# Gate and up side by side through Strassen's seven products in an encoder layer's two feed-forward blocks

## The chip, the cores and the metric

One NeuronCore of a Trainium2 chip runs the whole kernel. The metric is device time in microseconds (us) of one launch. TensorE (PE) multiplies matrices and writes its sums to PSUM, eight banks of 128 partitions x 512 fp32 in this kernel's use; VectorE (DVE) and ScalarE (ACT) do elementwise work; GpSimd (POOL) has a little of it; SyncE (SP) issues nearly all transfers.

## The reference

One encoder layer over 256 tokens of width 2048, in fp32: a feed-forward half-step, a mixer (attention and a Fourier branch), and a second feed-forward half-step. The two feed-forward steps are what the change is about:

```python
h = x + 1/2 * RMSNorm_post(SwiGLU(RMSNorm_pre(x)))     # D_MODEL = 2048, D_FF = 5632

def _rms_norm(x, g):
    y = xf * lax.rsqrt(jnp.mean(xf * xf, axis=-1, keepdims=True) + EPS)
    return y * g

def _swiglu(x, w_gate, w_up, w_down):
    return (jax.nn.silu(x @ w_gate) * (x @ w_up)) @ w_down
```

## The kernel before, in words

**Split products.** Every fp32 factor is cut into a high part (rounded to the fp32r type, by a copy on ACT, line 101) and a low part (the rest, by a subtraction on DVE, line 102); both lines are the helper `split`. A product is three matmuls (`mm3`, lines 106 to 108): high x high, high x low, low x high. The token side (128x128) is the stationary operand, the weight side (128x512) the moving one.

**Tokens.** 256 tokens are two tiles, t = 0 and 1. `u[t]` holds the transposed, gained but not yet normed input of a block, high and low part, 16 k-tiles of 128x128 each. The norm factor `rs[t]` is a number for each token and is applied after the product.

**Weights.** A weight piece is two k-tiles of 128x512: 512 KB, loaded into one of 5 raw buffers (`wraw`), split into one of 6 ring slots (`wring`). A ring slot comes free when the last matmul that reads it is done, a raw buffer when its split is done.

**The feed-forward loop (`ffn`).** The inner width 5632 is 11 blocks f of 512. For each f, `col_block` makes the gate product (16 k-tiles x 2 token tiles x 3 matmuls = 96 matmuls) and then the up product (96 more), each into two PSUM tiles `pc`. ACT takes the Silu of the gate (L445), DVE multiplies it by up (L447): `h`. After that `row_block` of the block before, f - 1, runs (96 matmuls for the four column parts of the down product into PSUM tiles `pr`, added to `y` by DVE at L219). Ahead of its fourth part, `turn_h` puts in eight transposes of `h` on PE (L177) into `pt`, which `split` turns into `hTh` and `hTl`, the stationary operands of the next `row_block`. The last block goes through `last_rows`, with the norm after the block and the transposed input of the next stage in an order written out by hand.

**What sets the order.** The kernel is traced in program order; a planner that runs ahead of time with its own estimates of durations then fixes the order of each engine's instructions and of the transfer queue, and hands out buffers. It takes what is ready, the earlier traced first. `tc.issue_after(ins)` pins instructions behind `ins` on `ins`'s engine, for work that would be ready too soon.

**Buffers.** `b8` has 8 buffers of 8 KB a partition for whole-width tiles (`y`, `h`, gains, mixer tiles); `upool` holds the four tiles of `u`; `chunk` has 3 pairs of 4 KB (`hT` and others); `wk` has 8 of 2 KB. PSUM is two pools, `pmm` with 5 banks for sums and `ptr` with 3 for transposes and small products.

Of the kernel before, what the change touches and what calls it, by code (L numbers as in the profile page):

```python
# [10 lines left out]
F32 = mybir.dt.float32  # L11
# [7 lines left out]
P = 128  # L19
D = 2048  # L20
# [25 lines left out]
SPARE_NEXT = ("b8", None, None, None)  # L46
B8 = 8
CH = 3
# [6 lines left out]
def encoder_layer(  # L55
    ctx: ExitStack,
    tc: tile.TileContext,
    x, xgT,
    f1_gate, f1_up, f1_down, f1_post,
    mix_pre, w_in, w_f, b_gate, q_g, k_g, w_ao, w_fo, w_fn, w_out, mix_post,  # L60
    f2_pre, f2_gate, f2_up, f2_down, f2_post,
    rope_cos, rope_sin, dft_pos, dft_ch, dft_ones, dft_mid, ident_in,
# [7 lines left out]
    b8 = pool("b8", B8)  # L70
    upool = pool("upool", 1)
# [51 lines left out]
    def pieces(src, spare=None):  # L123


        whole = {}

        def part(k0):
            if spare in (None, "chunk"):
                return piece(src, k0, WP, (chunk, "ch_hi", "ch_lo") if spare else None)  # L130
            if not whole:
                for c in ("h", "l"):
                    shape = [P, CK, NB]
                    whole[c] = big("w" + c, F32R, shape) if spare == "b8" else \
                        upool.tile(shape, F32R, tag=f"u{c}1", name=f"w{c}u")
# [38 lines left out]
    def transpose4(src, hi_dst, lo_dst):  # L174
        pt = ptr.tile([P, 4, P], F32, tag="tr", name="pt")
        for j in range(4):
            T.transpose(pt[:, j, :], src[:, j * P:(j + 1) * P], ident[:])  # L177
        split(hi_dst, lo_dst, pt[:])
# [5 lines left out]
    def new_u(t):  # L184
        return tuple(upool.tile([P, KD, P], F32R, tag=f"u{c}{t}", name=f"u{c}{t}") for c in "hl")

# [241 lines left out]

    def ffn(u, rs, wg, wu, wd, y, tail, gate0, w_next=None, early=()):

        nblk = F // NB
        prev = None
        for f in range(nblk):
            if f == 4:
                norm, nxt = tail()
            if f == 0:
                pg = gate0()
            else:
                pg = col_block(u, wg, f)
            pu = col_block(u, wu, f, between=early if f == 0 else ())  # L440
            ch = new_chunk("hT")
            hs = []
            for t in range(NT):
                sg = work("sg")
                A.activation(sg[:], pg[t][:], AF.Silu, scale=rs[t][:, 0:1])  # L445
                h = work("h")
                V.scalar_tensor_tensor(out=h[:], in0=pu[t][:], scalar=rs[t][:, 0:1], in1=sg[:],  # L447
                                       op0=ALU.mult, op1=ALU.mult)
                hs.append(h)

            def turn_h(ch=ch, hs=hs):
                for t in range(NT):
                    ts = slice(t * P, (t + 1) * P)
                    transpose4(hs[t], ch[0][:, :, ts], ch[1][:, :, ts])

            if prev is None:
                turn_h()
            else:
# [33 lines left out]

    def residual(t):
        h[t] = big(f"h{t}")
        load(h[t][:], x[t * P:(t + 1) * P, :])
        junk = big("junk8")
        ssq = small("ssx", 1)
        A.activation(junk[:], h[t][:], AF.Square, accum_out=ssq[:])
        rs[t] = rsqrt(ssq[:], 1, 1.0 / D, f"r{t}")

    y = [big(f"y{t}") for t in range(NT)]

    def tail():
# [3 lines left out]
    pk, nxt = ffn(u, rs, f1_gate, f1_up, f1_down, y, tail, gate0, w_in[4],  # L507
                  early=[lambda t=t: residual(t) for t in range(NT)])
    u, rs = nxt.u, nxt.rs
# [56 lines left out]
    def fold_tokens(b):  # L566

        a, e, o = work("ua"), work("ue"), work("uo")
        A.activation(a[:], cbs(nxt.y[0], b), AF.Copy, scale=rs[0][:, 0:1])
        for dst, op in ((e, ALU.add), (o, ALU.subtract)):  # L570
            V.scalar_tensor_tensor(out=dst[:], in0=cbs(nxt.y[1], b), scalar=rs[1][:, 0:1], in1=a[:], op0=ALU.mult, op1=op)
        bs = slice(4 * b, 4 * b + 4)
        for n, src in enumerate((e, o)):
            pt = ptr.tile([P, 4, P], F32, tag="tr", name="pt")
# [47 lines left out]
    def fold_f(k):  # L622

        if k == 0:
            pfold[0] = pmm.tile([P, NB], F32, tag="mm", name="pe")
            pfold[1] = ptr.tile([P, NB], F32, tag="tr", name="pe")
        if k + F_AHEAD < KD:
# [33 lines left out]
    def fourier_positions(b):  # L661

        zh, zl = workr("zh", [P, EW]), workr("zl", [P, EW])
        split(zh[:], zl[:], zs[b])
        pa = ptr.tile([P, NB], F32, tag="tr", name="pa")
# [9 lines left out]
        po = ptr.tile([P, NB], F32, tag="tr", name="pa")  # L675
# [12 lines left out]
    def fourier_channels(b, i, a):  # L688
# [3 lines left out]
        if j == 0:  # L692
            foT.append(new_chunk("foT"))
            pmid[0] = ptr.tile([P, NB], F32, tag="tr", name="pn")
        pb = ptr.tile([P, NB], F32, tag="tr", name="pb")
        c = slice(i * WO, (i + 1) * WO)
# [34 lines left out]
    def attn_scores(j, ch, t, ps):  # L731
# [3 lines left out]
        for hh in range(2):  # L735
            sc = ptr.tile([P, 2, S], F32, tag="tr", name="sc")
            for i in range(2):
# [16 lines left out]
    def attn_parts(j, ps, ch):  # L754
# [3 lines left out]
        def turn_p(hh, i):  # L758
            pt = ptr.tile([P, NT, S], F32, tag="tr", name="pt")
            for kt in range(NT):  # L760
# [6 lines left out]
        def values(hh, i, ph, pl):  # L767
            if i == 0:
                po[hh] = ptr.tile([P, 2, S], F32, tag="tr", name="po")
            js = slice(j * HD, (j + 1) * HD)  # L770
# [143 lines left out]

    y = [big(f"yf{t}") for t in range(NT)]

    def store(t, lo, n):
        nc.sync.dma_start(out[t * P:(t + 1) * P, lo:lo + n], h2[t][:, lo:lo + n])

    ffn(nxt.u, nxt.rs, f2_gate, f2_up, f2_down, y,  # L920
        lambda: (PostNorm(y, h2, bcast(f2_post, "gpost3"), 0.5, store), None), lambda: pg, early=[nxt.finish])

# [80 lines left out]


def _rows(w):
    k, n = w.shape
# [40 lines left out]
```

## Time and profile before

| | |
|---|---|
| median of 3 runs | 2079.43 us (2076.99 to 2079.51) |
| the profiled execution | 2076.99 us, span 2075.2 us, granted TensorE clock 0.999 |
| PE busy | 2053.8 us (99%), 9466 matmuls and transposes |
| DVE, ACT busy | 1317.2 us (63%), 1008.1 us (49%) |
| POOL busy | 50.9 us (2%) |
| moved by DMA | 411.11 MB, mean 198 GB/s |
| stages | first feed-forward block to about 745 us, mixer to about 1340 us, second feed-forward block to the end |

Busy time is a sum over the span; the length of a matmul record is its latency, and consecutive ones overlap, so PE's rate is read from the distance between starts.

### The profile page before, as it was taken

What the parts mean: (1) busy time and instruction counts of PE and PEld (TensorE: products, weight loads), DVE (VectorE), ACT (ScalarE), POOL (GpSimd) and SP (SyncE); (2) the same over time, 40 slices, a digit from 0 to 9 for tenths busy, and PEclk for the clock granted to TensorE, in tenths of its full rate; (3) what the DMA queues carried; (4) which work ended last, traced back from release to release, by engine and by line L of the source; (5) the groups of instructions that cost most, each with busy time, mean ns of one, the idle gap of its engine ahead of it and who ended that gap; (6) DMA issues with size and microseconds to landing.
All of it is one profiled execution on the core that took longest, in us unless ns stands there. A gap on an engine that the chain in (4) does not pass through costs nothing.

```text
span 2075.2 us, 25220 instructions
## 1 busy us (share of the span) xinstructions
PE 2053.8 (99%) x9466; PEld 1702.6 (82%) x9466; DVE 1317.2 (63%) x1682; ACT 1008.1 (49%) x1336; POOL 50.9 (2%) x46
## 2 busy tenths in 40 slices
PE   9999999999999999999999999999999999999998
PEld 7888888888888878888888888788888888888886
DVE  6545555555555698887877895864555555555556
ACT  7444444444444556556666654555444444444443
POOL 0000000000000020100000000200000000000002
PEclk9999999999999999999999999999999999999999
DMA  8665555555655686964555557466565555655553
GB/s 320 216 222 189 190 191 193 191 189 187 194 193 190 214 260 203 263 199 140 191 191 182 186 183 274 164 192 205 192 196 189 193 190 186 195 191 190 193 193 103
DMA packets 117867, 411.11 MB, mean 198 GB/s; under 512 B 12872, under 2 KB 19024, under 8 KB 116336
## 3 DMA queue, kind: packets, MB, share of 16 engines
q1 hardware_dynamic: 113392, 405.36, 59.3%
q0 software_dynamic: 4352, 4.13, 1.4%
q8 instruction: 74, 1.21, 0.2%
q14 instruction: 49, 0.40, 0.1%
HBM read 405.25 MB, written 4.19 MB: 197 GB/s over the span
## 4 chain that ended last, share of the span: by engine, by line
PE 94%; DVE 4%; DMA 1%; ACT 1%; issue 0%; SPq 0%; DVEq 0%; ACTq 0%
PE pc L107 19%; PE pc L108 19%; PE pc L106 19%; PE pr L106 10%; PE pr L107 10%; PE pr L108 10%; PE pt L177 1%; DVE wlo L102 1%; DMA raw<-in_w_fo 1%; DVE h L390 0%; PE pe L106 0%; PE pe L108 0%; PE pe L107 0%; PE pt L762 0%; PE pf L108 0%
## 5 line engine op out<-in xcount | busy, mean ns | idle before, releaser
L102 DVE TENSOR_TENSOR wlo<-raw,whi 128x1024 fp32r<-128x1024 f32 (+1 forms) x711 | 866.5, 1222 | 669.7 <-ACT whi L101 668.3
L101 ACT ACTIVATE whi<-raw 128x1024 fp32r<-128x1024 f32 (+1 forms) x711 | 751.2, 1059 | 874.8 <-PE pc L108 527.2
L106 PE MATMUL pc<-whi,uh 128*128 128x512 f32 x1840 | 719.3, 391 | 1.3 <-ACT uh L485 1.3
L107 PE MATMUL pc<-wlo,uh 128*128 128x512 f32 x1840 | 717.0, 390 | 2.2 <-DVE wlo L102 2.2
L108 PE MATMUL pc<-whi,ul 128*128 128x512 f32 x1840 | 717.2, 390 | 1.9 <-DVE ul L102 1.9
L108 PEld LDWEIGHTS pc<-whi,ul 128*128 128x128 f32 x1840 | 345.5, 188 | 74.4 <-DVE ul L102 3.0
L107 PEld LDWEIGHTS pc<-wlo,uh 128*128 128x128 f32 x1840 | 345.5, 188 | 73.4 <-DVE wlo L102 3.7
L106 PEld LDWEIGHTS pc<-whi,uh 128*128 128x128 f32 x1840 | 345.7, 188 | 73.0 <-ACT uh L485 2.7
L106 PE MATMUL pr<-whi,hTh 128*128 128x512 f32 x688 | 269.4, 392 | 0.0
L108 PE MATMUL pr<-whi,hTl 128*128 128x512 f32 x688 | 267.8, 389 | 0.0
L107 PE MATMUL pr<-wlo,hTh 128*128 128x512 f32 x688 | 267.8, 389 | 0.0
L108 PEld LDWEIGHTS pr<-whi,hTl 128*128 128x128 f32 x688 | 129.2, 188 | 26.9
L107 PEld LDWEIGHTS pr<-wlo,hTh 128*128 128x128 f32 x688 | 129.3, 188 | 26.1
L106 PEld LDWEIGHTS pr<-whi,hTh 128*128 128x128 f32 x688 | 129.2, 188 | 26.1
L219 DVE TENSOR_TENSOR yf<-pr,yf 128x512 f32<-128x512 f32 (+1 forms) x82 | 55.2, 674 | 10.3 <-PE pr L108 9.7
L219 DVE TENSOR_TENSOR y<-pr,y 128x512 f32<-128x512 f32 x80 | 54.8, 686 | 4.1 <-PE pr L108 3.6
L106 PE MATMUL pr<-whi,oTh 128*128 128x512 f32 x128 | 50.3, 393 | 0.0
L108 PE MATMUL pr<-whi,oTl 128*128 128x512 f32 x128 | 50.0, 390 | 0.0
L107 PE MATMUL pr<-wlo,oTh 128*128 128x512 f32 x128 | 49.9, 390 | 0.0
L106 PE MATMUL pr<-whi,mTh 128*128 128x512 f32 x120 | 46.9, 390 | 0.0
L108 PE MATMUL pr<-whi,mTl 128*128 128x512 f32 x120 | 46.7, 389 | 0.0
L107 PE MATMUL pr<-wlo,mTh 128*128 128x512 f32 x120 | 46.7, 389 | 0.0
(300 smaller groups left out, 1365.1 us busy)
## 6 DMA issues: line engine op xcount, KB each, us to landing
raw<-in_f_up SPq DMA_DIRECT2D x176, 512.0 KB, 4.6
raw<-in_f_down SPq DMA_DIRECT2D x176, 512.0 KB, 4.5
raw<-in_f_gate SPq DMA_DIRECT2D x175, 512.0 KB, 4.4
raw<-in_w_in SPq DMA_DIRECT2D x112, 512.0 KB, 4.8
raw<-in_w_ao SPq DMA_DIRECT2D x32, 512.0 KB, 3.9
raw<-in_w_out SPq DMA_DIRECT2D x32, 512.0 KB, 4.0
fraw<-in_w_f SPq DMA_DIRECT2D x16, 512.0 KB, 5.8
raw<-in_w_fo SPq DMA_DIRECT2D x16, 512.0 KB, 4.3
```

What stands on the lines that cost most here:

```text
L101: a = A.activation(hi, src, AF.Copy)
L102: v = V.tensor_tensor(out=lo, in0=src, in1=hi.bitcast(F32), op=ALU.subtract)
L106: T.matmul(ps, lh, rh, start=first, stop=False)
L107: T.matmul(ps, lh, rl, start=False, stop=False)
L108: return T.matmul(ps, ll, rh, start=False, stop=last)
L177: T.transpose(pt[:, j, :], src[:, j * P:(j + 1) * P], ident[:])
L219: V.tensor_tensor(out=dst, in0=ps, in1=dst, op=ALU.add)
```

## The change

From f = 2 on (`PLAIN = 2`), gate and up of a block are made together by `swiglu`. The 16 k-tiles are 4 chunks (kg) of 4. In chunks 0, 1 and 2 (`BY_SEVEN`) the first two k-tiles form, with the two token tiles and the two matrices, a 2x2 by 2x2 block product, made with seven products in place of eight (Winograd's form, with sums of factors on both sides and sums of results). The other two k-tiles of those chunks, and chunk 3, go as before. Blocks f = 0 and 1, the down product and the mixer's products stay as they are.

- **Token side, once for each feed-forward block.** `Forms` applies `rs` to `u` beforehand (`rows`: two transposes turn it into a row), makes the seven factors of each of the three chunks and splits them; it is put into block f = 1. The forms stay in six `b8` buffers until the last block.
- **Weight side, in every block.** From two raw pieces (`ra` = b11, b12 and `rb` = b22, b21) DVE makes w1 and w3 in a scratch tile `t13`, and overwrites b12 by w2 and b21 by w4: four more 128x512 operations. Seven factors are split, not four: ring slots (w1, w3), (w22, w21), (w11, w2), (w4).
- **Results.** Eight PSUM tiles at once: p5, p7, p1, p6 hold products that several results share, summed over the three chunks; g0, g1, u0, u1 hold the rest and the plain products. At the end of chunk 2, ACT copies p1 and DVE makes four sums x1, x2, x3, x5; at the end of the block they are added to g and u.
- **Buffers.** One PSUM pool of 8 banks; `u` moves into `b8`, which has 12 buffers in place of 8, and `upool` goes. The residual is not kept through the block: x (in the first) is loaded again, h2 (in the second) is stored to DRAM and loaded again, both in `tail`, traced at f = 4.
- The weights of gate and up for f >= 2 lie interleaved in DRAM (`f1_gu`, `f2_gu`); a raw piece is 512 KB as before.

```diff
-B8 = 8
+B8 = 12
+PLAIN = 2
+BY_SEVEN = (0, 1, 2)
...
-    pmm = pool("pmm", 5, space=bass.MemoryType.PSUM)
-    ptr = pool("ptr", 3, space=bass.MemoryType.PSUM)
+    pmm = pool("pmm", 8, space=bass.MemoryType.PSUM)
...
+        def rows(self):
+            pt = pmm.tile([P, NT, P], F32, tag="mm", name="pt")
+            for t in range(NT):
+                b = work("b", [P, P])
+                V.tensor_scalar(out=b[:], in0=ident[:], scalar1=0.0, scalar2=self.rs[t][:, 0:1], op0=ALU.mult, op1=ALU.add)
+                T.transpose(pt[:, t, :], b[:], ident[:])
+            self.r = work("r", [P, S])
+            A.activation(self.r[:], pt[:].rearrange("p t c -> p (t c)"), AF.Copy)
+
+        def chunk(self, kg):
+            ks = slice(kg * CK, (kg + 1) * CK)
+            a = chunk.tile([P, CK, S], F32, tag="ch_hi", name="un")
+            for t in range(NT):
+                V.tensor_tensor(out=a[:, :, t * P:(t + 1) * P], in0=self.u[t][0][:, ks, :].bitcast(F32),
+                                in1=self.u[t][1][:, ks, :].bitcast(F32), op=ALU.add)
+            V.tensor_tensor(out=a[:], in0=a[:], in1=self.r[:].unsqueeze(1).to_broadcast([P, CK, S]), op=ALU.mult)
+            n = 0
+            if kg in BY_SEVEN:
+                n = 2
+                f = chunk.tile([P, 7, P], F32, tag="ch_lo", name="sf")
...
+                V.tensor_tensor(out=f[:, 3, :], in0=a21, in1=a22, op=ALU.add)
+                V.tensor_tensor(out=f[:, 4, :], in0=f[:, 3, :], in1=a11, op=ALU.subtract)
+                V.tensor_tensor(out=f[:, 5, :], in0=a11, in1=a21, op=ALU.subtract)
+                V.tensor_tensor(out=f[:, 6, :], in0=a12, in1=f[:, 4, :], op=ALU.subtract)
+                hi, lo = (x.rearrange("p (a b) -> p a b", b=P) for x in self.room(7 * P))
+                split(hi, lo, f[:])
...
+            split(hi, lo, a[:, n:, :])
...
+    def swiglu(forms, w):
+        ps = {n: pmm.tile([P, NB], F32, tag="mm", name="pc") for n in ("p5", "p7", "u0", "g0", "p1", "p6", "g1", "u1")}
...
+        for kg in range(KD // CK):
+            more = list(range(CK))
+            if kg in BY_SEVEN:
+                more = more[2:]
+                a11, a12, na22, s1, s2, s3, s4 = forms.seven[kg]
+                ra, rb = raw_piece(w[kg], 0), raw_piece(w[kg], 1)
+                b11, b12, b22, b21 = ra[:, 0, :], ra[:, 1, :], rb[:, 0, :], rb[:, 1, :]
+                t = chunk.tile([P, WP, NB], F32, tag=("ch_hi", "ch_lo")[kg % 2], name="t13")
+                with tc.issue_after(latest["V"]):
+                    V.tensor_tensor(out=t[:, 0, :], in0=b12, in1=b11, op=ALU.subtract)
+                    V.tensor_tensor(out=t[:, 1, :], in0=b22, in1=b12, op=ALU.subtract)
+                w1, w3 = ring(t[:])
+                w22, w21 = ring(rb[:])
+                V.tensor_tensor(out=b12, in0=b22, in1=t[:, 0, :], op=ALU.subtract)
+                w11, w2 = ring(ra[:])
+                V.tensor_tensor(out=b21, in0=b12, in1=b21, op=ALU.subtract)
+                w4, = ring(rb[:, 1:2, :])
+                end = kg == BY_SEVEN[-1]
+                mul("p5", s1, w1, end)
+                mul("p7", s3, w3, end)
+                mul("u0", s4, w22)
+                mul("g0", a12, w21)
+                mul("p1", a11, w11, end)
+                mul("p6", s2, w2, end)
+                mul("g1", na22, w4)
+                if end:
+                    x1, x2, x3, x5 = (work(n) for n in ("x1", "x2", "x3", "x5"))
+                    A.activation(x1[:], ps["p1"][:], AF.Copy)
+                    V.tensor_tensor(out=x2[:], in0=ps["p6"][:], in1=x1[:], op=ALU.add)
+                    V.tensor_tensor(out=x3[:], in0=ps["p7"][:], in1=x2[:], op=ALU.add)
+                    V.tensor_tensor(out=x2[:], in0=ps["p5"][:], in1=x2[:], op=ALU.add)
+                    V.tensor_tensor(out=x5[:], in0=ps["p5"][:], in1=x3[:], op=ALU.add)
+                pieces_ = [(more, "g", 2), (more, "u", 3)]
+            else:
+                pieces_ = [(more[0:2], "g", 0), (more[0:2], "u", 1), (more[2:4], "g", 2), (more[2:4], "u", 3)]
+            for ks, c, i in pieces_:
+                for k, b in zip(ks, ring(raw_piece(w[kg], i)[:])):
+                    k += kg * CK
+                    for t in range(NT):
+                        mul(c + str(t), forms.plain[k][t], b, k == KD - 1)
+        hs = []
+        for t, (g, up) in enumerate(((x1, x2), (x3, x5))):
+            V.tensor_tensor(out=g[:], in0=ps[f"g{t}"][:], in1=g[:], op=ALU.add)
+            A.activation(g[:], g[:], AF.Silu)
+            V.tensor_tensor(out=up[:], in0=ps[f"u{t}"][:], in1=up[:], op=ALU.add)
+            V.tensor_tensor(out=up[:], in0=up[:], in1=g[:], op=ALU.mult)
+            hs.append(up)
+        return hs
...
+        forms = Forms(u, rs)
         for f in range(nblk):
             if f == 4:
-                norm, nxt = tail()
+                norm, nxt = tail(y)
...
+                    pg = col_block(u, wg, f, between=[forms.rows, lambda: forms.chunk(0), lambda: forms.chunk(1)])
+                    pu = col_block(u, wu, f, between=[lambda: forms.chunk(2), lambda: forms.chunk(3)])
...
+                hs = swiglu(forms, wgu[f - PLAIN])
...
+    def tail(y):
+        for t in range(NT):
+            h[t] = big(f"h{t}")
+            load(h[t][:], x[t * P:(t + 1) * P, :])
         g_post, g_pre = bcast(f1_post, "gpost1"), bcast(mix_pre, "gpre1")
```

More of the change, by code (lines that the diff above doesn't have):

```diff
@@ L133, in part @@
                     shape = [P, CK, NB]
-                    whole[c] = big("w" + c, F32R, shape) if spare == "b8" else \
-                        upool.tile(shape, F32R, tag=f"u{c}1", name=f"w{c}u")
+                    whole[c] = big("w" + c, F32R, shape)
             raw = wraw.tile([P, WP, NB], F32, tag="raw", name="raw")
@@ L174, in transpose4 @@
     def transpose4(src, hi_dst, lo_dst):
[L175 removed]
+        pt = pmm.tile([P, 4, P], F32, tag="mm", name="pt")
         for j in range(4):
@@ L184, in new_u @@
     def new_u(t):
-        return tuple(upool.tile([P, KD, P], F32R, tag=f"u{c}{t}", name=f"u{c}{t}") for c in "hl")
+        return tuple(big(f"u{c}{t}", F32R, [P, KD, P]) for c in "hl")
     def col_block(u, w, nb, between=(), at=()):
@@ new lines, in ring, with raw_piece, mul @@
+    def ring(src):
+        hi = wring.tile([P, WP, NB], F32R, tag="hi", name="whi")
+        lo = wring.tile([P, WP, NB], F32R, tag="lo", name="wlo")
+        n = src.shape[1]
+        split(hi[:, 0:n, :], lo[:, 0:n, :], src)
+        return [(hi[:, i, :], lo[:, i, :]) for i in range(n)]
+    def raw_piece(src, i):
+        raw = wraw.tile([P, WP, NB], F32, tag="raw", name="raw")
+        load(raw[:], src.rearrange("p (i k c) -> p i k c", k=WP, c=NB)[:, i])
+        return raw
+    def swiglu(forms, w):
+        ps = {n: pmm.tile([P, NB], F32, tag="mm", name="pc") for n in ("p5", "p7", "u0", "g0", "p1", "p6", "g1", "u1")}
+        begun = set()
+        def mul(n, a, b, last=False):
+            mm = mm3(ps[n][:], *a, *b, n not in begun, last)
+            begun.add(n)
+            return mm
+        for kg in range(KD // CK):
[31 more added lines that the diff above has]
+                pieces_ = [(more, "g", 2), (more, "u", 3)]
+            else:
+                pieces_ = [(more[0:2], "g", 0), (more[0:2], "u", 1), (more[2:4], "g", 2), (more[2:4], "u", 3)]
[12 more added lines that the diff above has]
+        return hs
@@ L441, in ffn @@
             ch = new_chunk("hT")
[L442 to L449, printed above, removed]
             def turn_h(ch=ch, hs=hs):
@@ L457, in ffn @@
                 turn_h()
+                y = [big(yname + str(t)) for t in range(NT)]
             else:
@@ L664, in fourier_positions @@
         split(zh[:], zl[:], zs[b])
-        pa = ptr.tile([P, NB], F32, tag="tr", name="pa")
+        pa = pmm.tile([P, NB], F32, tag="mm", name="pa")
         for i in range(2):
@@ L758, in turn_p @@
         def turn_p(hh, i):
-            pt = ptr.tile([P, NT, S], F32, tag="tr", name="pt")
+            pt = pmm.tile([P, NT, S], F32, tag="mm", name="pt")
             for kt in range(NT):
@@ L1002, in _cols, with _pairs @@
         w.reshape(k // (CK * P), CK, P, n // NB, NB).transpose(3, 0, 2, 1, 4)).reshape(n // NB, k // (CK * P), P, CW)
+def _pairs(g, u):
+    cut = lambda w: w[:, PLAIN * NB:].reshape(KD // CK, CK, P, -1, NB).transpose(3, 0, 2, 1, 4)
+    g, u = cut(g), cut(u)
+    seven = [g[..., 0, :], u[..., 0, :], u[..., 1, :], g[..., 1, :], g[..., 2, :], g[..., 3, :], u[..., 2, :], u[..., 3, :]]
+    plain = [g[..., 0, :], g[..., 1, :], u[..., 0, :], u[..., 1, :], g[..., 2, :], g[..., 3, :], u[..., 2, :], u[..., 3, :]]
+    out = np.stack(plain, 3)
+    for kg in BY_SEVEN:
+        out[:, kg] = np.stack([a[:, kg] for a in seven], 2)
+    return np.ascontiguousarray(out).reshape(*out.shape[:3], 2 * CW)
 def _rows(w):
```

96 lines of the change are left out of this document (67 added, 29 removed).

## The prediction, made before the changed kernel ran

> **What bounds the kernel now.** I read the page's busy shares first, then the chain that ended last, then the groups and the waits, and last the stretches and the order of time of one feed-forward period, where the change lies.
>
> ```profile
> span 2075.2 us, 25220 instructions
> PE 2053.8 (99%) x9466; PEld 1702.6 (82%) x9466; DVE 1317.2 (63%) x1682; ACT 1008.1 (49%) x1336; POOL 50.9 (2%) x46
> PE 94%; DVE 4%; DMA 1%; ACT 1%; issue 0%; SPq 0%; DVEq 0%; ACTq 0%
> ...
> L102 DVE TENSOR_TENSOR wlo<-raw,whi 128x1024 fp32r<-128x1024 f32 (+1 forms) x711 | 866.5, 1222 | 669.7 <-ACT whi L101 668.3
> L101 ACT ACTIVATE whi<-raw 128x1024 fp32r<-128x1024 f32 (+1 forms) x711 | 751.2, 1059 | 874.8 <-PE pc L108 527.2
> L106 PE MATMUL pc<-whi,uh 128*128 128x512 f32 x1840 | 719.3, 391 | 1.3 <-ACT uh L485 1.3
> ...
> 508.86 0.87 PE pt L177 x8
> 575.03 0.87 PE pt L177 x8
> ...
> 508.86:575.03 66.17, 66.17 (x298) 54.90 (x297) 36.64 (x37) 27.70 (x28) 0.00 (x0) 1.00 0.60 191
> 745.00:1340.00 595.00, 588.45 (x2897) 491.17 (x2896) 477.00 (x749) 355.07 (x604) 25.56 (x21) 1.00 0.63 203
> ```
>
> The chain is 94% PE. Its line 177 pieces (the transposes of `h`) mark a feed-forward period: 575.03 - 508.86 = 66.17 us, with PE busy for all of it. The groups say why the others do not matter: the low-part subtraction (L102) waits for ACT's copy, and that copy waits 527 us for PE, which has not yet given a ring slot back. A period holds 288 matmuls and eight transposes, so a matmul costs (66.17 - 0.87) / 288 = **0.2267 us** of PE's time; the 391 ns of its record is latency. VectorE is busy for 36.64 us of 66.17 (fifth column of the stretch), ScalarE for 27.70. The mixer's 595 us have 6.5 us without PE; the change touches only its PSUM pool.
>
> **The change part by part.** The sum is made against the profiled execution, 2076.99 us (its span and 1.8 us around it), which lies 2.4 us under the median shown, 2079.43.
>
> *1. Matmuls removed.* A chunk with seven products has 7 + 8 = 15 products for 16: three matmuls fewer. Three chunks, nine blocks (f = 2 to 10), two feed-forward parts: 3 x 3 x 9 x 2 = 162 matmuls, x 0.2267 = **-36.7 us**. A changed period should be 66.17 - 9 x 0.2267 = 64.13 us. Four transposes in `rows` add 4 x 0.87 / 8 = +0.4 us.
>
> *2. VectorE and ScalarE in a changed period.*
>
> ```profile
> L219 DVE TENSOR_TENSOR y<-pr,y 128x512 f32<-128x512 f32 x80 | 54.8, 686 | 4.1 <-PE pr L108 3.6
> L808 DVE TENSOR_TENSOR raw<-raw 128x512 f32<-128x512 f32 x16 | 11.0, 687 | 3.4 <-DMA raw<-in_w_fo 3.4
> L102 DVE TENSOR_TENSOR hTl<-pt,hTh 128x512 fp32r<-128x512 f32 x44 | 28.3, 683 | 0.3 <-ACT hTh L101 0.3
> L101 ACT ACTIVATE hTh<-pt 128x512 fp32r<-128x512 f32 x44 | 23.8, 589 | 1.8 <-PE pt L177 1.7
> ...
> 508.62 1.22 DVE L102 TENSOR_TENSOR wlo<-raw,whi 128x1024 fp32r<-128x1024 f32 x1 [1.76 <-ACT whi L101]
> 509.76 0.68 DVE L219 TENSOR_TENSOR y<-pr,y 128x512 f32<-128x512 f32 x1
> 510.37 1.22 DVE L102 TENSOR_TENSOR wlo<-raw,whi 128x1024 fp32r<-128x1024 f32 x1
> 511.50 1.28 DVE L102 TENSOR_TENSOR hTl<-pt,hTh 128x512 fp32r<-128x512 f32 x2
> 512.70 0.68 DVE L219 TENSOR_TENSOR y<-pr,y 128x512 f32<-128x512 f32 x1
> 516.10 0.68 DVE L219 TENSOR_TENSOR y<-pr,y 128x512 f32<-128x512 f32 x1
> ```
>
> A seven-chunk asks of VectorE four sums of weights (4 x 0.687, from the SBUF-to-SBUF row L808), three full low parts and one half (3 x 1.222 + 0.683) and two full ones for its plain tiles: 2.75 + 4.35 + 2.44 = 9.5 us, while PE works 45 x 0.2267 = 10.2 us on it. The plain chunk asks 4.9; the end of the block ten operations on 128x512 (x2, x3, x2, x5, two each for g, up and the product), 6.9; the down part 8 x 1.222 + 8 x 0.686 + 2 x 0.683 = 16.6. Together 28.6 + 4.9 + 6.9 + 16.6 = 57.0 us of 64.13, or 89%, where it is 55% now. ScalarE gets 3 x (1.059 + 0.589) + 0.6 = 5.5 us more, 33 of 64. Cost on the path: nothing, as long as VectorE's work stays ahead. The cover is the ring. In a seven-chunk the six slots hold one whole chunk; the slot of (w1, w3) is back 6 matmuls = 1.4 us into a chunk and its successor is due 10.2 us in, so the next chunk's copy (1.06), low part (1.22) and the two sums before them (1.4) have 8.8 us. Going through a chunk in VectorE's queue, in order, I find its pieces ready some 4 us before they are due. If this cover were gone, each us lost in a chunk would count 54 times.
>
> [...] Where nothing waits, starts on VectorE are closer than the records are long: 509.76 - 508.62 = 1.14 us behind a record of 1.22, and 0.61 behind one of 0.68. So a seven-chunk really takes about 4 x 0.61 + 5 x 1.14 + 0.61 = 8.75 us, 86% of PE's 10.2. [...]
>
> *3. The start of each changed block.* The sums (t13) of chunk 0 are pinned behind the last split traced, which is `hTl` of token tile 1.
>
> ```profile
> 508.47 1.02 PEld L177 LDWEIGHTS pt<-ident,h 128*128 128x128 f32 x8
> 514.80 0.19 PEld L106 LDWEIGHTS pc<-whi,uh 128*128 128x128 f32 x1
> 508.89 1.06 ACT L101 ACTIVATE whi<-raw 128x1024 fp32r<-128x1024 f32 x1 [0.30 <-PE pr L108]
> 509.86 1.07 ACT L101 ACTIVATE hTh<-pt 128x512 fp32r<-128x512 f32 x2
> 513.86 1.06 ACT L101 ACTIVATE whi<-raw 128x1024 fp32r<-128x1024 f32 x1 [2.93 <-PE pr L108]
> 515.22 1.06 ACT L101 ACTIVATE whi<-raw 128x1024 fp32r<-128x1024 f32 x1 [0.30 <-PE pr L108]
> ```
>
> Now `hTl` ends at 511.50 + 1.28 = 512.78 and the next block's matmuls begin at 514.80. With the same order after the change: one addition (0.6) and two sums (1.3) to 514.7, ACT's copy of (w1, w3) to 515.8, its low part to 517.0, where PE wants the low part at 515.0. That is a wait of about 2 us; over 18 blocks 36 us, the whole gain. Against it stands that the products of (w22, w21), 6 matmuls or 1.4 us, do not depend on the sums, nor do 18 plain ones (u0, u1 and then g0) behind them, 4.1 us; the planner takes what is ready, so it can put these first. The bounds are 0 and 2.0 us a block (0 and 36 us). I take 0.4, near the lower end, since 5.5 us of independent work covers a delay of 2: **+7 us**. Queued behind the pinned sums on VectorE are the addition for the last down tile (it started at 516.10, 1.3 us behind the block's start) and with it the PSUM bank that the eighth sum, u1, needs about 8 us into the block: covered.
>
> *4. PSUM.* A block's sums take all 8 banks. Four (p5, p7, p1, p6) come back after chunk 2, 24 + 48 matmuls = 16 us before the down part begins, which then has four to turn over, each filled in 12 matmuls = 2.7 us and emptied in 0.69. The other four come back after four additions, 2.8 us. Cost 0. In the mixer one pool of 8 in place of 5 and 3 can shorten or lengthen waits; PE has 6.5 us of idle time there, so I bound it by -3 and +6 and take 0.
>
> *5. Forms in block f = 1.*
>
> ```profile
> L556 DVE TENSOR_TENSOR tmp<-q,gsq 128x256 f32<-128x256 f32 x16 | 6.0, 419 | 0.0
> L486 DVE SCALAR_TENSOR_TENSOR ul<-xt,uh 128x128 fp32r<-128x128 f32 x32 | 9.2, 347 | 0.0
> ```
>
> For each seven-chunk: two additions of 512 (1.37), one product of 1024 (1.22), four operations on 128x128 (under 0.35 each by L486, which has a pointer operand more; 1.3), low parts of 896 and 512 (1.1 + 0.68): 5.7 us; the plain chunk 3.8. In all 21 us on top of 36.6, so 58 of 66 us; no stall on the average. But the first two chunks can come as a burst of 11 us, traced ahead of weights that the ring wants; six slots hold 6 x 12 x 0.2267 = 16 us of PE's work, of which some 13.6 are ahead. Bounds 0 and 3 us a part; I take 1: **+2 us**.
>
> *6. Transfers.*
>
> ```profile
> h<-in_x SPq DMA_DIRECT2D x2, 1024.0 KB, 9.3
> GB/s 320 216 222 189 190 191 193 191 189 187 194 193 190 214 260 203 263 199 140 191 191 182 186 183 274 164 192 205 192 196 189 193 190 186 195 191 190 193 193 103
> SPq L82 <- DVE wlo L102: 1549.8, 663, 19.2
> ```
>
> The residual's reload and the gains, up to four loads of 1 MB, become possible when `u` is given back, at the end of f = 1's up product, and the transfer queue, which mostly waits for raw buffers, will issue them at once: 4 MB at the 320 GB/s of the first slice is 13 us in which weights stand behind them. By then the ring (16 us) and one or two raw pieces cover it, and the down part of block 0 has 22 us before the first changed block. Bounds 0 and 5 us a part; I take 1: **+2 us**. The spill of h2 is as far off the path as the spill of h in the kernel before.
>
> Sum: 2077.0 - 36.7 + 0.4 + 7 + 2 + 2 = 2051.7; I say **2051**.
>
> **The rivals.**
>
> *Everything is hidden.* The start of a block is filled with ready products, transfers and forms are covered: 2077.0 - 36.7 + 0.4 = 2041, and with 3 us from the pool 2038. For it: VectorE's and ScalarE's waits today are all for PE. Against: 89% is far from 55%.
>
> *Raw buffers hold back the sums.* `ra` and `rb` are kept until w2 and w4 are split, not for one copy and one subtraction; four pieces of five buffers are taken by one chunk. By the queue of part 2 the buffer for the next `rb` is free 8.5 us into a chunk, the transfer takes 4.4 us and the sums want it after 12.9: no margin. A slip of 0.5 us that is not made up, in each of 54 chunks, is 27 us; with it and nothing for part 3 the time is 2041 + 27 + 2 = 2070.
>
> ```profile
> raw<-in_f_gate SPq DMA_DIRECT2D x175, 512.0 KB, 4.4
> ```
>
> *VectorE and ScalarE starve PE inside a chunk (slower).* The seven factors make a ladder: sums, copy, low part, then w2 = b22 - t, copy, low part, then w4, copy, low part. Where no other work fills VectorE's time during the three copies (1.06 + 1.06 + 0.59 = 2.7 us) a chunk costs it 9.5 + 2.7 = 12.2 us against PE's 10.2, so 2.0 x 54 = 108 us: 2041 + 108 = 2149; half of it gives 2095. It decides from 36.3 / 54 = 0.67 us a chunk on. For it: the order is fixed beforehand and VectorE cannot step around a wait, and in the fullest rows the 1.2 us records leave little room. Against: a next chunk's plain low parts, and that of rb, need no sums and lie in between; the slack of 4 us is met again in each chunk.
>
> **How the numbers follow.** The forecast (2043 to 2062, between nothing and 1.1 us at each block's start) gets 0.55; everything hidden (2036 to 2043) 0.13; raw buffers or another slip of some tenths a chunk (2062 to 2080) 0.15; starving (above 2080) 0.17. The range 2038 to 2077 leaves out the last and the edges of two. A change of 0.2% (4.2 us) is about what a measurement of this kernel can tell from none. Faster by more: 0.55 + 0.13 + 0.11 = 0.79; within: 0.04; slower: 0.17.
>
> **What would show it.** Part 1: each of the three `pc` rows loses 54 matmuls, and the distance between two groups of transposes falls to 64.1 us plus the waits. Part 2: VectorE busy for about 57 us of it. Part 3: PE idle in the first microseconds of each changed block, with the low part as releaser, and either (w22, w21) or (w1, w3) first in its order. Parts 5 and 6: a longer period f = 1, or idle PE at the first changed block. The prediction is wrong if PE's idle time recurs in every chunk: if it waits for L102 the ladder is the cause, if L102's chain ends at a transfer, the raw buffers.

## The result, and the profile after

| | median (us) | runs | ratio to before, 95% interval |
|---|---|---|---|
| before, same chip | 2078.21 | 4 | |
| changed | 2102.25 (2101.6 to 2103.05) | 4 | 1.0116 [1.0098, 1.0133] |

The change costs 24 us where 26 were forecast as a gain. The profiled execution of the changed kernel took 2101.8 us, span 2100.0, granted clock 0.993. Its page, in the lines that answer to those of before (share and count by engine, the chain, then groups with busy us and mean ns, then idle time before them and its releaser):

```profile
span 2100.0 us, 25662 instructions
PE 2056.3 (98%) x9308; PEld 1670.8 (80%) x9308; DVE 1655.3 (79%) x2216; ACT 1094.2 (52%) x1490; POOL 50.8 (2%) x46
PE 45%; DVE 9%; ACT 3%; issue 1%; DMA 0%; ACTq 0%; DVEq 0%
...
L101 ACT ACTIVATE whi<-raw 128x1024 fp32r<-128x1024 f32 (+1 forms) x765 | 763.6, 1024 | 488.4 <-PE pc L108 149.6
...
L101 ACT ACTIVATE whi<-t 128x1024 fp32r<-128x1024 f32 x54 | 57.3, 1061 | 133.5 <-DVE t L516 133.5
L101 ACT ACTIVATE hTh<-pt 128x512 fp32r<-128x512 f32 x44 | 24.1, 595 | 165.2 <-PE pt L176 165.1
```

The matmuls did go: 9308 = 9466 - 162 + 4. The chain is followed back only to 856 us this time (its shares add up to 58%), and of these 58 DVE and ACT have 12, where they had 5 of 100 before. ACT's copies now wait for the sums `t` (L516, 54 times) and for `pt`; before, they mostly waited for PE to give back a ring slot. The transposes of each stage say where the time went (start in us of a group on PE, in each kernel's own trace):

| group of eight transposes | before | changed |
|---|---|---|
| of `h`, block f = 1 of the first part | 111.66 | 112.17 |
| of the last block, f = 10, of the first part | 707.22 | 708.18 |
| of `yo`, end of the mixer | 1330.65 | 1348.05 |
| of `h`, block f = 1 of the second part | 1441.63 | 1465.92 |

The nine changed periods of the first part take 596.0 us where they took 595.6: the gain of 18 us is given back inside the periods. The mixer is 16.4 us longer and the way from it to the second part's block f = 1 is 6.9 us longer. The sum against 2076.99: +0.5 - 36.7 (matmuls) + 37.6 (given back in 18 periods) + 23.3 = 2101.7. So there are two losses to explain, in different places.

**First place: the seven-product chunks, from the start of a block.** The order of time of the changed kernel (start, length, engine, line, operation; in brackets the idle time before it and what ended it), and in a fence of its own the stretch of that period (PE, PEld, DVE, ACT, POOL busy, then clock):

```profile
1531.98 1.03 PE L176 MATMUL pt<-ident,x 128*128 128x128 f32 x8
...
1598.25 1.03 PE L176 MATMUL pt<-ident,x 128*128 128x128 f32 x8
1598.88 1.09 ACT L101 ACTIVATE hTh<-pt 128x512 fp32r<-128x512 f32 x2 [10.21 <-PE pt L176]
1599.51 1.29 DVE L102 TENSOR_TENSOR hTl<-pt,hTh 128x512 fp32r<-128x512 f32 x2 [0.38 <-ACT hTh L101]
1600.72 0.68 DVE L515 TENSOR_TENSOR t<-raw 128x512 f32<-128x512 f32 x1
1602.10 1.06 ACT L101 ACTIVATE whi<-t 128x1024 fp32r<-128x1024 f32 x1 [2.12 <-DVE t L516]
...
1604.58 0.39 PE L106 MATMUL pc<-whi,fh 128*128 128x512 f32 x1
...
1608.71 0.69 DVE L102 TENSOR_TENSOR wlo<-raw,whi 128x512 fp32r<-128x512 f32 x1 [0.76 <-ACT whi L101]
1608.73 0.19 PEld L106 LDWEIGHTS pc<-whi,fh 128*128 128x128 f32 x1 [0.32 <-ACT whi L101]
...
1609.46 0.19 PEld L107 LDWEIGHTS pc<-wlo,fh 128*128 128x128 f32 x1 [0.54 <-DVE wlo L102]
...
1611.94 0.68 DVE L515 TENSOR_TENSOR t<-raw 128x512 f32<-128x512 f32 x1
...
1622.54 0.68 DVE L515 TENSOR_TENSOR t<-raw 128x512 f32<-128x512 f32 x1
```

```profile
1598.40:1664.70 66.30, 65.79 (x290) 52.70 (x288) 53.38 (x62) 31.67 (x35) 0.00 (x0) 1.00 0.57 190
```

In the kernel before, DVE split weights at 508.62 and ACT at 508.89, around the transposes at 508.86 and ahead of `hTh` at 509.86. Now ACT stands idle for 10.21 us, nothing of the next block is prepared, and the first sums come right behind `hTl`. PE begins the block on time (1604.58, 0.23 us behind the last matmul of the down part) and first waits 4.15 us later, for w4, the last factor of the chunk (the 128x512 forms). From there a chunk takes 1611.94 to 1622.54 = 10.60 us on VectorE, with bubbles such as 0.76 us behind ACT's copies, and PE needs 10.2: the block starts without a lead and makes none. The distances between PE's starts above 0.2267 us add up to some 0.9, 0.4 and 0.7 us in the three chunks of this period; in each, the first of these waits is for w4. The waits of the changed kernel (total us, times, longest) show it on PE's side:

```profile
ACT hTh L101 <- PE pt L176: 165.1, 18, 10.2
PEld pc L107 <- DVE wlo L102: 36.2, 79, 1.5
PEld pc L106 <- ACT whi L101: 19.9, 52, 0.4
```

18 is the number of changed blocks. The weight loads' waits are what to read here: the stretch has PE busy for 65.79 of 66.30 us, because a matmul's record (0.39) is longer than its pace (0.2267) and covers a gap of 0.16.

**Second place: the mixer.** Stretches of the changed kernel, then one of the kernel before, and PE's order of time in the changed one:

```profile
752.00:766.00 14.00, 9.59 (x38) 7.29 (x38) 11.33 (x46) 7.02 (x19) 1.10 (x1) 0.76 0.89 316
1018.00:1042.00 24.00, 19.75 (x91) 17.05 (x91) 19.34 (x40) 15.14 (x28) 0.00 (x0) 0.86 0.45 144
...
745.00:1358.00 613.00, 595.99 (x2901) 497.69 (x2900) 480.47 (x751) 354.66 (x604) 25.55 (x21) 0.99 0.62 200
```

```profile
752.00:766.00 14.00, 13.28 (x64) 10.23 (x63) 13.15 (x27) 10.39 (x19) 1.38 (x2) 1.00 0.89 300
```

```profile
755.21 0.66 PE L176 MATMUL pt<-ident,y 128*128 128x128 f32 x4 [1.95 <-DVE y L403]
756.70 1.08 PE L176 MATMUL pt<-ident,y 128*128 128x128 f32 x4 [0.83 <-DVE gsq L664]
759.40 1.11 PE L176 MATMUL pt<-ident,y 128*128 128x128 f32 x4 [1.62 <-DVE y L403]
760.17 0.77 PE L106 MATMUL pc<-wh,uh 128*128 128x512 f32 x1
760.74 0.63 PE L107 MATMUL pc<-wl,uh 128*128 128x512 f32 x1
```

PE waits for transposes' inputs with nothing in between, and then runs slower: a group of four transposes 1.08 us instead of 0.66, a matmul 0.63 instead of 0.39. By the long stretches PE is idle for 613.00 - 595.99 = 17.0 us, 10.5 more than before (6.5 of 595); the other 7.5 are longer busy time for the same work, which a mean clock of 0.99 over 613 us (6 us) about accounts for.

### The profile page after: what moved, and what is told of

Read it like the earlier page. It is cut to its first block, busy times and chain, and to the rows that moved or that the text cites. A ratio compares the mean times of both kernels' runs of the same rounds, so it can differ in the third digit from the quotient of the medians.

```text
span 2100.0 us, 25662 instructions
## 1 busy us (share of the span) xinstructions
PE 2056.3 (98%) x9308; PEld 1670.8 (80%) x9308; DVE 1655.3 (79%) x2216; ACT 1094.2 (52%) x1490; POOL 50.8 (2%) x46
## 4 chain that ended last, share of the span: by engine, by line
PE 45%; DVE 9%; ACT 3%; issue 1%; DMA 0%; ACTq 0%; DVEq 0%
PE pc L107 8%; PE pc L108 8%; PE pc L106 7%; PE pr L106 6%; PE pr L108 6%; PE pr L107 6%; DVE wlo L102 5%; ACT whi L101 2%; PE pt L176 1%; DVE yf L218 1%; DVE raw L521 0%; DMA raw<-in_w_fo 0%; DVE h L389 0%; DVE yo L403 0%; PE pt L895 0%
## 5 line engine op out<-in xcount | busy, mean ns | idle before, releaser
L102 DVE TENSOR_TENSOR wlo<-raw,whi 128x1024 fp32r<-128x1024 f32 (+1 forms) x765 | 892.9, 1182 | 218.5 <-ACT whi L101 214.1
L107 PE MATMUL pc<-wlo,fh 128*128 128x512 f32 x1098 | 435.7, 397 | 8.8 <-DVE wlo L102 8.8
L108 PE MATMUL pc<-whi,fl 128*128 128x512 f32 x1098 | 428.3, 390 | 0.0
L106 PE MATMUL pc<-whi,fh 128*128 128x512 f32 x1098 | 418.5, 395 | 0.0
L106 PE MATMUL pc<-whi,uh 128*128 128x512 f32 x688 | 271.2, 394 | 0.9 <-ACT uh L617 0.9
L107 PE MATMUL pc<-wlo,uh 128*128 128x512 f32 x688 | 268.8, 391 | 2.1 <-DVE wlo L102 2.1
L108 PE MATMUL pc<-whi,ul 128*128 128x512 f32 x688 | 268.8, 391 | 1.8 <-DVE ul L102 1.8
L108 PEld LDWEIGHTS pc<-whi,fl 128*128 128x128 f32 x1098 | 206.2, 188 | 40.4
L108 PEld LDWEIGHTS pc<-whi,ul 128*128 128x128 f32 x688 | 129.2, 188 | 29.6 <-DVE ul L102 2.6
L107 PEld LDWEIGHTS pc<-wlo,uh 128*128 128x128 f32 x688 | 129.2, 188 | 28.9 <-DVE wlo L102 3.7
L106 PEld LDWEIGHTS pc<-whi,uh 128*128 128x128 f32 x688 | 129.4, 188 | 27.6 <-ACT uh L617 2.3
```

The source lines that it names most:

```text
L102: v = V.tensor_tensor(out=lo, in0=src, in1=hi.bitcast(F32), op=ALU.subtract)
L106: T.matmul(ps, lh, rh, start=first, stop=False)
L107: T.matmul(ps, lh, rl, start=False, stop=False)
L108: return T.matmul(ps, ll, rh, start=False, stop=last)
```

## The experiments

Two theories, one for each place. *Lead*: the sums of chunk 0 come too late, and VectorE's 10.6 us a chunk can't win back what PE lacks. *Pool*: the one PSUM pool alone costs the mixer its time. Rivals: VectorE's added work itself is too much (the ladder); the swiglu's 8 banks or the forms upset the mixer.

**1. The pool.** `b_pool8` is the kernel before with nothing but the pool changed; `a_split53` is the changed kernel with the two pools back.

```diff
 b_pool8 (from the kernel before)
-    pmm = pool("pmm", 5, space=bass.MemoryType.PSUM)
-    ptr = pool("ptr", 3, space=bass.MemoryType.PSUM)
+    pmm = pool("pmm", 8, space=bass.MemoryType.PSUM)
...    every ptr.tile(..., tag="tr") -> pmm.tile(..., tag="mm")
 a_split53 (from the changed kernel): the reverse of this, and in swiglu
+        ps = {n: pmm.tile([P, NB], F32, tag="mm", name="pc") for n in ("p5", "p7", "u0", "g0", "p1")}
+        ps.update({n: ptr.tile([P, NB], F32, tag="tr", name="pc") for n in ("p6", "g1", "u1")})
```

> The kernel before with its two PSUM pools (5 and 3 banks) made one of 8, nothing else. In the changed kernel the mixer alone is 18 us longer and the way into the second feed-forward block 7 us, both without any of the seven products. If the shared pool is the cause (the planner gives transposes and sums the same banks and orders PE's work otherwise), this kernel takes 2078 + 18 to 25 = 2096 to 2103 us, and its mixer shows idle gaps of 4 us or so with a lowered granted clock behind them. If the cause is that u and h2 moved into other SBUF buffers, or the transfers of h2 and x, it stays at 2078.

> The changed kernel with the PSUM banks in two pools of 5 and 3 again (the eight sums of a block take 5 of the one and 3 of the other). If the shared pool costs the mixer its time: 2102 - 18 to 25 = 2077 to 2084 us, the feed-forward periods still at 66.25 us. If SBUF buffers or transfers are the cause: 2102. If the split makes the eight sums of a block wait for banks, the periods grow above 66.25.

`b_pool8`: **2099.92 us, ratio 1.0111 [1.0094, 1.0128]**. The pool alone costs 22 us (against 2078.05, the kernel before on the same chip) in a kernel that has no Strassen product at all. Its stretches have the same gaps and the same clock as the changed kernel's:

```profile
752.00:766.00 14.00, 9.27 (x36) 6.94 (x36) 11.31 (x45) 6.76 (x18) 1.10 (x1) 0.76 0.87 313
745.00:1358.00 613.00, 595.85 (x2902) 497.38 (x2901) 480.61 (x752) 354.69 (x605) 25.57 (x21) 0.99 0.62 198
```

`a_split53`: **2078.27 us, 1.0001 [0.9992, 1.0011]**. The mixer's time is back, the periods are not: 66.26 us between these.

```profile
1508.51 1.03 PE L177 MATMUL pt<-ident,x 128*128 128x128 f32 x8
1574.77 1.03 PE L177 MATMUL pt<-ident,x 128*128 128x128 f32 x8
```

**2. The pin.** The sums issue after the last split *of a weight* (`latest["W"]`, set where a weight is split), no longer after `hTl` (in the diff: the pin itself, and the line that is added where weights are split); with the one pool (`a_pin`) and with two (`a_pin_split53`).

```diff
-                with tc.issue_after(latest["V"]):
+                with tc.issue_after(latest["W"]):
...
+        latest["W"] = latest["V"]
```

> The changed kernel with the sums of weights pinned behind the last split of a weight piece, not behind the split of the transposed h. Theory of the ring: pieces go through the ring in the order traced, so that while the first sums wait for h's split nothing behind them can be prepared; the ring runs empty at each block's start and the chunks behind it live from hand to mouth. Then the periods fall from 66.25 to about 64.2 us, 18 of them: 2102 - 36 = 2066 us. Rival, the ladder: a chunk takes VectorE and ScalarE 10.6 us (distance between the first sums of two chunks in the trace) against PE's 10.2 whatever the start, so the 0.4 us in each of three chunks stays and only the start's 0.9 us goes: periods 65.4, 2102 - 16 = 2086 us.

> Both at once: the earlier pin and the two PSUM pools. If ring and pool are the two causes and independent: 2102 - 36 - 25 = 2041 to 2048 us, 1.5 to 1.8% below the kernel before. With the ladder in place of the ring: about 2061. If the effects overlap or one is wrong, it lies at the better of the two single kernels.

**2093.49 us, 1.0074 [1.0059, 1.0089]**, and **2068.69 us, 0.9956 [0.9941, 0.9971]**: 9 us each, a quarter of what the lead is worth by experiment 3. Neither reading in the two expectations gave that. The periods of `a_pin_split53` are 65.73 us, and its sums are still not early:

```profile
1568.84 1.09 ACT L102 ACTIVATE hTh<-pt 128x512 fp32r<-128x512 f32 x2 [10.21 <-PE pt L178]
1569.01 0.68 DVE L519 TENSOR_TENSOR t<-raw 128x512 f32<-128x512 f32 x1
```

They now follow the start of `hTh` by 0.17 us, though the raw pieces had been issued 18 us before, at 1551.04. Something that `hTh` frees or takes holds them. `t13` of chunk 0 has the tag `ch_hi`, the one of `hTh`, which gave the next theory: buffers of one tag are handed out in traced order, so `t13` can't have one before `hTh`, traced earlier, has had its own.

**3. Is the lead enough, or is VectorE's work too much?** `a_early` is `a_split53` with chunk 0's factors traced earlier: the lines from `ra, rb = ...` to `w4, = ...` become a function, called for block f + 1 in `turn_h`, ahead of the transposes of `h`. `a_nosums` keeps the order of `a_split53` and leaves out the four sums of weights (t13, w2 and w4), so that w1 to w4 are plain weights. `a_early_gsums` is `a_early` with the four sums on GpSimd.

```diff
 a_early
+            def turn_h(ch=ch, hs=hs, f=f):
+                nonlocal made
+                if PLAIN <= f + 1 < nblk:
+                    made = factors(wgu[f + 1 - PLAIN], 0)
...
+                w1, w3, w22, w21, w11, w2, w4 = made if kg == 0 else factors(w, kg)
 a_nosums
-                w1, w3 = ring(t[:])
+                w1, w3 = ring(ra[:])
...    the four V.tensor_tensor left out
```

> Two PSUM pools as in a_split53, and the factors of a block's first chunk traced ahead of the transposes of h, so that the scratch tile of the sums takes its buffer ahead of hT (the pin is then behind the last weight split by itself). In a_pin_split53 the pin was moved alone and the first sums still ran behind h's split: buffers of one tag seem to be given in the order traced. Theory of the lost lead: with the first factors made during the down product the ring is full at the block's start; three chunks of 10.6 us on VectorE against 10.2 on PE then use up 1.2 us of about 10 us of lead and PE does not wait: periods 64.2 to 64.4, 2078 - 18 x 1.9 = 2044 us. Rival, the ladder in each chunk delays PE whatever the lead: periods 65.7 as in a_pin_split53, 2069 us.

> a_split53 with the four sums of weights of each seven-chunk left out (the products run on the wrong weights; loads, splits, matmuls are all there). VectorE has 2.4 us less in each chunk, and no split waits for a sum. Both theories of the chunk say that PE then waits for nothing: periods 64.13, 2078 - 18 x 2.1 = 2041 us. If the periods stay above 65, the sums are not the cause, and the ring's extra pieces, the eight PSUM sums or the raw buffers are.

> a_early with the four sums on GpSimd, which is idle here. Its 128x512 operations took 1.43 us in the profile before (gain times y), so 5.7 us a chunk, beside 6.7 us of VectorE's. If VectorE's load is what delays chunks: 2041 to 2044 us, and no better than a_early if that one waits for nothing. If the two engines get in each other's way (VectorE's records longer than 1.22 us), or the longer ladder (2.9 us for the first two sums) is late: 2050 to 2090.

`a_early`: **2043.15 us, 0.9837 [0.9821, 0.9852]**; `a_nosums`: **2043.63 us, 0.9834 [0.982, 0.9849]**; `a_early_gsums`: **2041.82 us, 0.9831 [0.9815, 0.9847]**. The three agree within their error. With a lead the sums cost nothing, leaving them out brings no more than having them early, and moving them off VectorE (DVE 1562.9 us busy where `a_early` has 1653.2) brings nothing that can be told. So the ladder by itself isn't the cause. This rests on `a_early`, which keeps the ladder in every chunk; `a_nosums` takes away the pin and the scratch tile along with the sums, so that alone it couldn't tell lead from ladder. From the order of time of `a_early`, the transposes and the sums, now 8.8 us ahead of `hTh`; then the weight loads' waits for the low part (36.1 us, 81 times in `a_split53`):

```profile
1490.35 1.03 PE L177 MATMUL pt<-ident,x 128*128 128x128 f32 x8
1554.48 1.03 PE L177 MATMUL pt<-ident,x 128*128 128x128 f32 x8
...
1546.45 0.69 DVE L501 TENSOR_TENSOR t<-raw 128x512 f32<-128x512 f32 x1
1555.27 1.07 ACT L102 ACTIVATE hTh<-pt 128x512 fp32r<-128x512 f32 x2
```

```profile
PEld pc L108 <- DVE wlo L103: 3.8, 6, 1.4
```

A period is 64.13 us, to the digit what part 1 of the prediction gave.

**4. Tag and pin apart.** `a_own6` is `a_pin_split53` with `t13` in a pool of its own; `a_own6_v` is the same with the pin of the changed kernel (behind `hTl`) again. The order in which things are traced is that of the changed kernel in both.

```diff
+    tpool = pool("tpool", 1)
-    wk = pool("wk", 8)
+    wk = pool("wk", 6)
...
-                t = chunk.tile([P, WP, NB], F32, tag=("ch_hi", "ch_lo")[kg % 2], name="t13")
+                t = tpool.tile([P, WP, NB], F32, tag="t13", name="t13")
```

> a_pin_split53 with the scratch tile t13 in a pool of its own (one buffer of 4 KB) in place of the tags it shares with hT; the pool wk pays for it with 6 buffers in place of 8. Theory, the shared tag holds the sums behind hT, since buffers of one tag are given out in traced order: the first sums of a block now start before hTh, the ring gets its lead, periods of 64.1 to 64.6 us, 2043 to 2052 in all. Rival, the order in which ring slots are given out or the order of the queue holds them: sums still behind hTh, periods of 65.7, 2069. Rival, the single buffer of t13 puts the chunks one behind another: periods of 66 and more, above 2072.

> a_own6 with the pin of the changed kernel again (sums behind the last split traced, hTl, on VectorE). Theory: the tag and the pin each hold the sums behind hT by themselves, so freeing the tag alone brings nothing: periods of about 66.2 us and 2076 to 2081, as a_split53. Rival, the tag alone was the cause and the pin is harmless once the tag is free: 2042 to 2050, periods of 64.2.

`a_own6`: **2041.76 us, 0.9826 [0.9812, 0.9841]**; `a_own6_v`: **2078.01 us, 1.0003 [0.9993, 1.0013]**. In microseconds gained over `a_split53`: the pin alone 9.6, the tag alone 0.3 (less than such medians differ by), both 36.5. Each is a hold by itself; whichever stands later decides. `a_own6`, then `a_own6_v`:

```profile
1548.10 0.68 DVE L520 TENSOR_TENSOR t<-raw 128x512 f32<-128x512 f32 x1
1556.91 1.07 ACT L103 ACTIVATE hTh<-pt 128x512 fp32r<-128x512 f32 x2
...
1565.32 0.69 DVE L520 TENSOR_TENSOR t<-raw 128x512 f32<-128x512 f32 x1
1575.91 0.68 DVE L520 TENSOR_TENSOR t<-raw 128x512 f32<-128x512 f32 x1
```

```profile
1574.96 1.29 DVE L104 TENSOR_TENSOR hTl<-pt,hTh 128x512 fp32r<-128x512 f32 x2 [0.37 <-ACT hTh L103]
1576.16 0.68 DVE L520 TENSOR_TENSOR t<-raw 128x512 f32<-128x512 f32 x1
```

In `a_own6` a chunk still takes VectorE 1575.91 - 1565.32 = 10.59 us. The 0.4 us that it loses to PE in each of three chunks are 1.2 us a block, which the lead pays; it must be earned back in the plain chunk and the down part, where VectorE has less to do than PE (4.9 of 10.9 us and 16.6 of 22.6 by part 2's terms).

**5. Are the two losses independent?** `a_early_pool8` is `a_early` with the one pool of 8 banks.

> a_early with the one PSUM pool of 8 banks of the changed kernel. Theory: the two causes are independent, the pool costs its 22 us in the mixer and on the way into the second feed-forward part, whatever the feed-forward blocks do: 2043.2 + 22 = 2065, periods of 64.1 us as in a_early. Rival, the pool of 8 is needed or harmless once the ring has its lead: 2043 to 2048. Rival, with one pool the planner also spoils the lead: above 2075 with periods over 65 us.

**2064.87 us, 0.9935 [0.9918, 0.9951]**: 21.7 us above `a_early`, as the pool costs 21.9 in `b_pool8`. They add.

**6. What in the one pool costs.** In the stretch 752 to 760 the kernel before runs other matmuls between the same transposes:

```profile
754.58 0.63 PE L177 MATMUL pt<-ident,y 128*128 128x128 f32 x4 [0.36 <-DVE y L404]
754.96 0.48 PE L106 MATMUL pc<-wh,uh 128*128 128x512 f32 x1
...
755.98 0.63 PE L177 MATMUL pt<-ident,y 128*128 128x128 f32 x4
```

In the changed kernel these `pc<-wh,uh` come at 760.17, behind the last transposes. That would be the rule of experiment 4 again, on PSUM: with one tag, a sum traced later can't have its bank before a transpose traced earlier, whose input is late. `b_turn_mm` tries this with both pools kept, 5 and 3: only `transpose4`'s tile moves to the tag of the sums.

```diff
-        pt = ptr.tile([P, 4, P], F32, tag="tr", name="pt")
+        pt = pmm.tile([P, 4, P], F32, tag="mm", name="pt")
```

> The kernel before with both PSUM pools, 5 and 3, but the transposes' tile pt of transpose4 taken from pmm, the pool and tag of the sums. Theory: what costs in the one pool is that transposes and sums share a tag, so that a sum traced later can't get its bank, and its matmuls can't run, while a transpose traced earlier still waits for its input; then the same gaps ahead of pt stand at 752 to 760 us (about 1.9, 0.8 and 2.0 us) and on the way into the second feed-forward part, with the half clock behind them: 2088 to 2101. Rival, the order of the small products (po, pa, pb, sc, the other tiles of ptr) or the number of banks makes the gaps: 2076 to 2082, and no gap above 0.5 us at 752 to 760.

**2090.4 us, 1.0063 [1.0046, 1.008]**: 13 us of the 22, from one tile. Two gaps of this size are there ahead of the same tile, not three:

```profile
751.75 1.12 PE L177 MATMUL pt<-ident,y 128*128 128x128 f32 x4 [1.82 <-DVE y L404]
...
760.10 0.63 PE L177 MATMUL pt<-ident,y 128*128 128x128 f32 x4 [2.11 <-DVE y L404]
```

Here the sums share five banks with the transposes, so a lack of banks could be blamed; in `b_pool8` they share eight, and the gaps are the same. The order that a shared tag imposes fits both, but it is inferred: no run keeps eight banks in one pool and gives the transposes a tag of their own. The other 9 us, such as the loss at 1018 to 1042, were not tried singly; the remaining tiles of `ptr` are the candidates.

## Why the prediction was wrong, point by point

Between the 2051.7 us of the sum and the 2101.7 found from the stages lie 50 us: 30.6 in the 18 changed periods (37.6 where part 3 had 7 and part 2 nothing) and 23.3 for the pool (part 4 had nothing), less 3.9 that parts 1, 5 and 6 took too high.

*Part 1, matmuls removed: right.* 162 went, at 0.2267 each; where nothing holds the ring a period is 64.13 us.

*Part 2, VectorE: the amount right, the cover wrong, the first step that failed.* VectorE is busy for 53.4 us of a period (57 by the sum of records, which overlap at their ends: the sum at 1600.72 begins 0.08 us before the end of `hTl`, 1600.80) and ScalarE for 31.7 (33). A chunk takes it 10.6 us, not 8.75, since it also stands behind ACT's copies for 0.3 to 0.8 us at a time. I had the pieces "ready some 4 us before they are due"; in the trace w4's low part ends at 1608.71 + 0.69 = 1609.40, and its weight load waited 0.54 us for it. That cover assumed a ring that is ahead at the start of a block; at 10.6 against 10.2 it can't get ahead on its own. Measured: 2.1 us a block, 37.6 in all, or 0.70 us for each of 54 chunks.

*Part 3, the start of a block: the right place, the wrong wait.* The pin does hold the sums behind `hTl`. But the wait whose ends I worked out as 0 and 2.0 us, PE's for the low part of (w1, w3), does not occur: `hTl` ends 2.6 us behind the first transpose (1600.80 against 1598.25), since ACT and DVE then have no weight to split, and the low part is done at 1604.48 (it began at 1603.26 and takes 1.22), just ahead of 1604.58. That the loss of 2.1 us a block is near my upper end is chance. Nor does anything step around the sums: ACT did not touch the ready `rb` until the copy of w1 and w3 was done, at 1603.06, though it had been idle for 2.12 us; no run changes this order by itself. What the sums' lateness costs is the lead of the ring, paid in the three chunks. What I missed besides is the second hold, the tag: the prediction names the pin only, and by experiment 4 the pin's removal alone would have left 27 us on the table.

*Part 4, PSUM: the second step that failed.* The bounds were -3 and +6, taken 0; it is +22. The bounds came from PE's idle time before (6.5 us), as if the order of work would stay. The one pool changes the order, by experiment 6 because it ties late transposes to later sums, and the lower clock adds to it (0.76 from 752 to 766, 1.00 in the kernel before).

*Parts 5 and 6, forms and transfers: small.* In `a_early` the transposes of block f = 1 come at 112.33 (111.66 before), the next two periods are 64.16 and 64.13, and block f = 1 of the second part is 111.2 us behind the mixer's end (111.0 before). Together about 1 us, where I took 4.

*The rivals.* "Everything is hidden" gave 2041 us: that is the time of the repaired kernels, 2041.8 to 2043.2. Raw buffers: ACT does wait for them (in `a_early` 33.8 us for `raw<-in_f_gu`), but with periods of 64.13 that is off the path. The slower rival was the ladder, and by its own sign it is what PE meets: the waits for L102 recur in every chunk, and 0.70 us a chunk is just over the 0.67 from which it decides. But it is not the 2.0 us that it reckoned, it costs nothing where the ring has a lead, and with two PSUM pools it ends at 2078 (`a_split53`); that the result lies above 2080 is the pool's doing. The range ended at 2077, 1 us under the kernel that has the lost lead alone; it had no room for the pool.

## What to carry to other kernels

Where a planner hands out buffers in traced order, a shared tag is a shared queue: a scratch tile that shares its tag with a late tile, or sums that share a bank pool with transposes, wait for whatever was traced before them. So when work is moved or pools are merged, ask of each new tile which earlier tile of its tag must be served first, and do not count on the planner to step around it. And a stage whose helper engines run 4% slower than PE (10.6 against 10.2 us a chunk) was free here where it started with a lead, and delayed PE in each of its chunks where it had none: look at who is idle just before the stage begins (here ACT, 10.21 us) before summing up busy time.

## What the runs showed of the hardware

In the two falls read here the granted clock went from 1.00 to 0.50 behind gaps of PE of 1.95 us at most. Stretches of 2.5 us of the changed kernel, from 752.5:

```profile
752.50:755.00 2.50, 0.76 (x4) 0.28 (x2) 2.00 (x4) 0.99 (x3) 0.00 (x0) 1.00 0.47 133
755.00:757.50 2.50, 1.46 (x8) 1.13 (x8) 1.99 (x6) 2.50 (x7) 0.00 (x0) 0.72 0.98 279
757.50:760.00 2.50, 0.88 (x5) 0.60 (x4) 2.50 (x7) 1.60 (x5) 0.00 (x0) 0.50 0.98 362
760.00:762.50 2.50, 2.50 (x9) 2.01 (x8) 2.01 (x9) 0.60 (x1) 0.05 (x1) 0.50 1.06 436
```

PE is busy for 0.76 and 1.46 of the first two stretches, its longest single gap is 1.95 us, and the clock is at 0.50 by 757.5 and still there at 762.5, 2.3 us after PE has begun to work without a pause (760.17). So with the gaps of 1.95 + 0.83 + 1.62 = 4.4 us some 2 us more were lost: 0.9 in the two slow groups of transposes, and six matmuls from 760.17 to 762.88 took 2.7 us, not 1.4. From the end of the last matmul at 753.26 (752.87 + 0.39) to the slow group at 756.70 are 3.4 us in which PE had only four transposes. `b_turn_mm` has a fall without transposes. Its last gap ahead of the fall, then two stretches:

```profile
748.97 0.50 PE L107 MATMUL pc<-wlo,uh 128*128 128x512 f32 x1 [1.01 <-DVE wlo L102]
```

```profile
747.50:750.60 3.10, 1.42 (x6) 0.52 (x4) 2.04 (x4) 0.00 (x0) 0.00 (x0) 1.00 1.05 245
750.80:753.30 2.50, 1.55 (x6) 1.46 (x7) 2.29 (x5) 1.58 (x5) 0.00 (x0) 0.50 0.69 257
```

Here the clock is at 0.50 by 750.80, behind one gap of 1.01 us and 0.9 us into the next (the last matmul ends at 749.93), and the last transposes lie over 9 us back (740.46). So this fall came with no gap as long as 1.95 us and no transpose beside it; how much idle time within what length it takes, no run here shows.
